# A decoder block on one core: in its first stage the low part of h is subtracted by VectorE from PSUM, GpSimd subtracts 256 columns at a time, and the adaLN sums are issued earlier

## The chip, the cores and the metric

The kernel runs on one core of a Trainium2 chip. The metric is the device time of one execution in microseconds. Before the change three runs gave 889.89, 890.54 and 891.4 us, median 890.54.

## What is computed

The reference is one decoder block for 512 tokens of width 1024, all in float32: RMS norm and adaLN modulation, a projection of width 6656 for two attention branches and their gates, block-sparse attention and retention in parallel, gated merging, output projection, a squared-ReLU MLP and a last RMS norm. The change concerns the first lines alone:

```python
c_act = jax.nn.silu(c)
ada = (c_act @ w_ada[l] + b_ada[l])[:, None, :]
sh1, sc1, g1, sh2, sc2, g2 = jnp.split(ada, N_ADA, axis=-1)
h = modulate(rms_norm(x, ln1_w[l]), sh1, sc1)   # h * (1 + scale) + shift
proj = h @ w_in[l]
mq, mk, mv, rq, rk, rv, rg, ga, gr = jnp.split(proj, split_at, axis=-1)
```

`w_ada` is 1024 x 6144, `w_in` 1024 x 6656.

## The kernel before

To keep float32 accuracy on TensorE, each matrix is split in two parts of type float32r: a high part, which is a rounded copy, and a low part, which is the matrix minus that copy. A product of two matrices is three products: high by high, high by low, low by high. Names that begin with `whi` and `wlo` are the parts of a weight, `hh{j}` and `hl{j}` those of h.

The first stage walks over the 8 chunks j of 128 columns of `x` (the loop `for j in range(NK)`, line 338). For every chunk it needs four things:

- **The modulation.** The 128 shifts and 128 scales of the chunk are columns of silu(c) @ w_ada. `load_ada` brings 1 MB of w_ada as tile `wada` in four loads of 256 KB (3 buffers). The product is taken on VectorE and ScalarE, not on TensorE: `ada_start` (line 261) lets ScalarE write the first two of eight weighted rows as `adaacc`, and `ada_sum` (line 268) adds the other six with VectorE, one instruction of 128 x 256 each (line 270), in two sums that alternate, and then adds the two (line 274). `ada_columns` (line 276) sums over the partitions with four small matmuls into the bank `O`: these are called the column sums below. `modulation` (line 283) makes `mod` of them on VectorE (lines 285 and 286).
- **h.** `transposed` (line 288) lets TensorE turn four 128 x 128 blocks of the normalised x into the bank `PT`, of which there is one. `h_tile` (line 297) lets ScalarE write h to an SBUF tile (line 299), then `hh` as a copy of it (line 224); the low part `hl` is subtracted by GpSimd (line 227, `POOL`), for the last chunk by VectorE.
- **The weights.** `load_first` brings 0.39 MB of w_in as `raw` (128 x 768, 3 buffers): the columns of v, and of the first pairs of heads of q and k. `w_split` (line 302) has `whi` copied by ScalarE (line 304) and `wlo` subtracted by GpSimd in one instruction of 768 columns (line 305). Elsewhere, in `load_w`, GpSimd subtracts 1024 columns in four pieces of 256 (line 187).
- **The products.** `product` (line 345) issues one of 18 matmuls: six outputs (four banks of v, one of q, one of k), each with hh by whi, hh by wlo, hl by whi.

PE, VectorE, ScalarE and GpSimd run this stage in the order in which the program is written (a manual schedule); the loads stand in the queue of SP. In round j, TensorE's order was: transposes of chunk j+1, six products hh by whi, three hh by wlo, the column sums of chunk j+1, three hh by wlo, six hl by whi. Behind the stage PE alone keeps a written order; the other engines' order there is set by a scheduler. The loads of the first pair of later weights (`first_pair`), the split of v (`moba_v`) and the rotary embedding of q and k (`rope`, `stack_q`, `stack_k`, tiles `sw`, `roped`, `sig`, `qs`, `kh`, `kl`) follow, then the attention's first scores (`moba_scores`, lines 563 and 564).

Of the kernel before, what the change touches and what calls it, by code (L numbers as in the profile page):

```python
# [8 lines left out]
F32 = mybir.dt.float32  # L9
F32R = mybir.dt.float32r  # L10
AF = mybir.ActivationFunctionType
ALU = mybir.AluOpType
AX = mybir.AxisListType

P = 128
D = 1024
S = 512
NT = S // P
NK = D // P
# [8 lines left out]
def block_kernel(  # L28
# [27 lines left out]
    ACT, DVE, POOL, PE = nc.scalar, nc.vector, nc.gpsimd, nc.tensor  # L56
# [26 lines left out]
    hh = [H.tile([P, S], F32R, name=f"hh{j}", tag=f"hh{j}") for j in range(NK)]  # L83
    hl = [H.tile([P, S], F32R, name=f"hl{j}", tag=f"hl{j}") for j in range(NK)]
    z_stack, Z = pool("Z", "right")
    vm_stack, VM = pool("VM", "right")
    st_stack, ST = pool("start")
# [54 lines left out]
    cact = G.tile([P, 8], F32, name="cact")  # L142
# [29 lines left out]
    def load_raw(parts):  # L172
# [2 lines left out]
            dma(view(raw), src)  # L175
        return raw

    def load_w(parts, lo_engine=None, pool=G):
        raw = load_raw(parts)
        hi = pool.tile([P, 1024], F32R, name="whi", tag="whi", bufs=4 if pool is G else 2)  # L180
        lo = pool.tile([P, 1024], F32R, name="wlo", tag="wlo", bufs=4 if pool is G else 2)
        ACT.activation(hi, raw, AF.Copy)  # L182
        eng = lo_engine or POOL

        for q in range(0, 1024, 256):
            qs = slice(q, q + 256)
            eng.tensor_sub(lo[:, qs], raw[:, qs], hi[:, qs].bitcast(F32))  # L187
        return hi, lo

    def v3(t, n):  # L190
# [10 lines left out]
    def load_pair(w, k0, ca, cb, lo_engine=None):  # L201

        hi, lo = load_w(
            [
                (lambda t: v3(t, 256)[:, :, 0:P], rows(w, k0, 4, ca, P)),
                (lambda t: v3(t, 256)[:, :, P:256], rows(w, k0, 4, cb, P)),
            ],
            lo_engine=lo_engine,
        )
        return v3(hi, 256), v3(lo, 256)  # L210
# [11 lines left out]
    def split(src, hi, lo, eh, el):  # L222
        if eh is ACT:
            ACT.activation(hi, src, AF.Copy)
        else:
            eh.tensor_copy(hi, src)  # L226
        return el.tensor_sub(lo, src, hi.bitcast(F32)).ins  # L227
# [19 lines left out]
    def load_ada(j):  # L247
        t = ST.tile([P, 8, 2, P], F32, name="wada", tag="wada", bufs=3)
        for k0, k1, i in ((0, 4, 0), (0, 4, 1), (4, 8, 0), (4, 8, 1)):
            dma(t[:, k0:k1, i, :], wada_v[:, k0:k1, i, j * P : (j + 1) * P])  # L250
        return t.rearrange("p k a n -> p k (a n)")

    def load_first(j):
        raw = G.tile([P, 1024], F32, name="raw", tag="raw", bufs=3)
        for c0, c1, src in ((0, 512, MV), (512, 640, MQ), (640, 768, MK)):
            dma(raw[:, c0:c1], w_in[j * P : (j + 1) * P, src : src + c1 - c0])
        hi = G.tile([P, 1024], F32R, name="whi", tag="whi", bufs=4)
        lo = G.tile([P, 1024], F32R, name="wlo", tag="wlo", bufs=4)
        return raw[:, :768], hi[:, :768], lo[:, :768]

    def ada_start(j):

        a = [ST.tile([P, 256], F32, name="adaacc", tag="adaacc", bufs=4) for _ in range(2)]
        for k in range(2):
            ACT.activation(a[k], ada[j][:, k, :], AF.Copy, scale=cact[:, k : k + 1])
        return a

    def ada_sum(j, a, ks, end=True):
        for k in ks:
            DVE.scalar_tensor_tensor(  # L270
                a[k % 2], ada[j][:, k, :], cact[:, k : k + 1], a[k % 2], op0=ALU.mult, op1=ALU.add
            )
        if end:
            DVE.tensor_add(a[0], a[0], a[1])  # L274

    def ada_columns(a):

        cp = ps("O")
        for i in range(2):
            PE.matmul(cp[:, 2 * i : 2 * i + 2], a[0][:, i * P : (i + 1) * P], ones32[:, 0:2], start=True, stop=True)  # L280
        return cp

    def modulation(j, cp):
        mod = ST.tile([P, 2], F32, name="mod", tag="mod", bufs=3)
        DVE.tensor_scalar(mod[:, 0:1], cp[:, 0:1], badac(0, j), None, op0=ALU.add)
        DVE.tensor_scalar(mod[:, 1:2], cp[:, 2:3], badac(1, j, True), ln1c(j), op0=ALU.add, op1=ALU.mult)
        return mod

    def transposed(j):
        tp = ps("PT")  # L290
        for t in range(NT):
            PE.transpose(tp[:, t * P : (t + 1) * P], xt[t][:, j * P : (j + 1) * P], ident)
            if j == 0:
                busy(3)
        return tp

    def h_tile(j, tp, mod):
        h32 = ST.tile([P, S], F32, name="h32", tag="h32", bufs=2)
        ACT.activation(h32, tp, AF.Identity, bias=mod[:, 0:1], scale=mod[:, 1:2])
        split(h32, hh[j], hl[j], ACT, POOL if j < NK - 1 else DVE)  # L300

    def w_split(j):
        raw, hi, lo = wf[j]
        ACT.activation(hi, raw, AF.Copy)
        POOL.tensor_sub(lo, raw, hi.bitcast(F32))

    for t in range(1, NT):
        load_x(t)
        if t == 2:
            load_params()  # L310
    ada, wf = [], []

    def load_step(j):
        ada.append(load_ada(j))
        wf.append(load_first(j))

    for j in range(2):
        load_step(j)
    for t in range(NT):
        ss = ST.tile([P, 1], F32, name="ss", tag="ss", bufs=4)  # L320
        ACT.activation(sq, xt[t], AF.Square, accum_out=ss)
# [5 lines left out]
    a = ada_start(0)  # L327
# [4 lines left out]
    tp = transposed(0)  # L332
    busy(4)
    cp = ada_columns(a)
    busy(3)
    mod = modulation(0, cp)
    w_split(0)
    a = ada_start(1)
    h_tile(0, tp, mod)
    for j in range(NK):  # L340
        _, hi, lo = wf[j]
        more = j + 1 < NK
        if j + 2 < NK:
            load_step(j + 2)

        def product(i, a, b, first, last):

            w = (hi, lo)[b]
            hx = (hh, hl)[a][j]
            if i < 4:  # L350
                PE.matmul(acc_mv[i], hx[:, i * P : (i + 1) * P], w[:, 0:512], start=first, stop=last)
            else:
                c0 = 512 if i == 4 else 640
                PE.matmul((acc_q0, acc_k0)[i - 4], w[:, c0 : c0 + P], hx, start=first, stop=last)

        if more:
            ada_sum(j + 1, a, range(2, 8))
            tp = transposed(j + 1)
        for i in range(6):
            product(i, 0, 0, j == 0, False)  # L360
        for i in range(6):
            product(i, 0, 1, False, False)
            if not more:
                product(i, 1, 0, False, True)
            elif i == 2:
                cp = ada_columns(a)
                mod = modulation(j + 1, cp)
        if more:
            w_split(j + 1)
            if j + 2 < NK:  # L370
                a = ada_start(j + 2)
            else:
                first_pair = [load_pair(w_in, k0, MQ + P, MK + P, eng) for k0, eng in ((0, POOL), (4, DVE))]
            h_tile(j + 1, tp, mod)
            for i in range(6):
                product(i, 1, 0, False, False)
    st_stack.close()
# [905 lines left out]
```

## Time and profile before

| what | value |
|---|---|
| median of 3 runs | 890.54 us |
| the profiled execution, its own time | 889.06 us |
| its span, first to last instruction | 887.0 us |
| mean granted TensorE clock | 0.993 |
| TensorE busy (PE) | 851.1 us, 96% of the span |
| VectorE (DVE), ScalarE (ACT), GpSimd (POOL) busy | 468.0, 408.7, 506.1 us |
| the first stage: first products, last products end | 19.2 us, 70.1 us |

All positions below are microseconds from the start of the span. A row of the timeline gives the start, the time until the end of the last instruction of the row, the engine, the line and operation, what is written from what is read, the number of instructions, and in brackets the idle time before it with what ended it. Instructions of one engine overlap by some 0.1 us, so four in a row take less than four times one. Matmuls overlap more: the rows say 0.39 us for a product of 512 columns, and their starts lie 0.23 us apart. PEclk is the granted clock as a share of 2.4 GHz.

### The profile page before, as it was taken

To read this page: it belongs to the slowest core of one execution; us is meant where nothing else is said; L and a number is where in the kernel's file an instruction comes from. 1 tells how busy PE (TensorE), PEld (TensorE's weight loads), DVE (VectorE), ACT (ScalarE), POOL (GpSimd) and SP (SyncE) were. 2 spreads that over 40 slices of the span, in tenths; PEclk is the share of its full clock that TensorE was granted. 3 is DMA by queue.
4 is the path that set the end of the run, shared out by engine and by line. 5 is a ranking of instruction groups with operands and counts; after the bars stand their busy time and mean duration, and the time that the engine had idled before them with its cause. 6 is when DMAs were issued, how large, how long until landed. Compare 5 with 4: busy or idle time off the path is not lost.

```text
span 887.0 us, 11777 instructions
## 1 busy us (share of the span) xinstructions
PE 851.1 (96%) x4138; PEld 708.8 (80%) x4138; DVE 468.0 (53%) x887; ACT 408.7 (46%) x697; POOL 506.1 (57%) x608
## 2 busy tenths in 40 slices
PE   7889999999999999999999889999999999999996
PEld 4667878779788988778888679888888888888885
DVE  5885676777787877973286786103304022222225
ACT  5457988887645637645232253323332211112125
POOL 4466353526544644655656375977777755555554
PEclk9999999999999999999999999999999999999999
DMA  9945222221354453422454732534433322222202
GB/s 280 297 143 173 65 77 66 96 72 48 119 157 141 120 160 103 147 80 89 132 181 152 251 114 90 156 97 127 137 98 93 113 95 96 97 99 99 107 28 95
DMA packets 104426, 108.41 MB, mean 122 GB/s; under 512 B 4832, under 2 KB 93232, under 8 KB 104368
## 3 DMA queue, kind: packets, MB, share of 16 engines
q1 hardware_dynamic: 104224, 107.41, 38.9%
q8 instruction: 32, 0.52, 0.3%
q14 instruction: 26, 0.21, 0.1%
q10 hardware_dynamic: 144, 0.26, 0.1%
HBM read 105.55 MB, written 2.10 MB: 121 GB/s over the span
## 4 chain that ended last, share of the span: by engine, by line
PE 63%; DVE 18%; ACT 8%; DMA 6%; issue 3%; POOL 1%; SPq 1%; ACTq 0%; DVEq 0%; POOLq 0%
PE ps_acc L218 16%; PE ps_acc L219 16%; PE ps_acc L220 16%; DMA ada_raw<-in_w_ada_dram 4%; DVE adaacc L270 3%; PE ps_S L220 2%; PE ps_S L219 2%; PE ps_S L218 2%; ACT sw L478 1%; DVE ada_acc L802 1%; DVE adaacc L274 1%; DMA wada<-in_w_ada_dram 1%; ACT whi L182 1%; DVE ada_acc L799 1%; DVE qs L502 1%
## 5 line engine op out<-in xcount | busy, mean ns | idle before, releaser
L187 POOL TENSOR_TENSOR wlo<-raw,whi 128x256 fp32r<-128x256 f32 x500 | 387.7, 808 | 254.3 <-ACT whi L182 221.7
L182 ACT ACTIVATE whi<-raw 128x1024 fp32r<-128x1024 f32 x126 | 132.4, 1057 | 186.0 <-PE ps_O L220 104.9
L218 PE MATMUL ps_acc<-hh,whi 128*128 128x512 f32 x304 | 121.5, 400 | 0.0
L220 PE MATMUL ps_acc<-hh,wlo 128*128 128x512 f32 x304 | 119.5, 393 | 0.0
L219 PE MATMUL ps_acc<-hl,whi 128*128 128x512 f32 x304 | 119.4, 393 | 0.0
L219 PE MATMUL ps_acc<-h2l,whi 128*128 128x512 f32 (+1 forms) x288 | 105.5, 366 | 0.9 <-POOL h2l L227 0.6
L218 PE MATMUL ps_acc<-h2h,whi 128*128 128x512 f32 (+1 forms) x288 | 105.5, 366 | 0.0
L220 PE MATMUL ps_acc<-h2h,wlo 128*128 128x512 f32 (+1 forms) x288 | 105.3, 366 | 0.0
L226 DVE CAST fh<-act 128x512 fp32r<-128x512 f32 x32 | 16.1, 509 | 132.5 <-PE ps_O L219 128.0
L220 PEld LDWEIGHTS ps_acc<-hh,wlo 128*128 128x128 f32 x304 | 57.4, 189 | 12.7
L219 PEld LDWEIGHTS ps_acc<-hl,whi 128*128 128x128 f32 x304 | 57.6, 190 | 10.2
L218 PEld LDWEIGHTS ps_acc<-hh,whi 128*128 128x128 f32 x304 | 57.6, 189 | 10.1
L219 PEld LDWEIGHTS ps_acc<-h2l,whi 128*128 128x128 f32 x288 | 54.3, 189 | 9.8 <-POOL h2l L227 0.8
L220 PEld LDWEIGHTS ps_acc<-h2h,wlo 128*128 128x128 f32 x288 | 54.3, 189 | 8.8
L218 PEld LDWEIGHTS ps_acc<-h2h,whi 128*128 128x128 f32 x288 | 54.3, 189 | 8.6
L219 PE MATMUL ps_acc<-wlo,fh 128*128 128x512 f32 (+1 forms) x136 | 52.1, 383 | 0.0
L220 PE MATMUL ps_acc<-whi,fl 128*128 128x512 f32 (+1 forms) x136 | 52.1, 383 | 0.0
L218 PE MATMUL ps_acc<-whi,fh 128*128 128x512 f32 (+1 forms) x136 | 52.1, 383 | 0.0
L799 DVE SCALAR_TENSOR_TENSOR ada_acc<-ada_raw,cact,ada_acc 128x256 f32<-128x256 f32 x48 | 32.9, 685 | 35.8 <-DMA ada_raw<-in_w_ada_dram 35.1
L1134 ACT ACTIVATE relu<-ps_acc 128x512 f32<-128x512 f32 x32 | 18.8, 587 | 66.0 <-PE ps_acc L220 64.5
L775 DVE TENSOR_TENSOR g<-g,ps_acc 128x256 f32<-128x256 f32 x8 | 3.4, 419 | 86.1 <-PE ps_acc L774 86.1
L1135 POOL TENSOR_TENSOR act<-relu 128x512 f32<-128x512 f32 x32 | 34.3, 1071 | 17.2 <-ACT relu L1134 17.2
(284 smaller groups left out, 1897.4 us busy)
## 6 DMA issues: line engine op xcount, KB each, us to landing
raw<-in_w_ff_dram SPq DMA_DIRECT2D x64, 512.0 KB, 3.3
raw<-in_w_in_dram SPq DMA_DIRECT2D x32, 512.0 KB, 3.7
ada_raw<-in_w_ada_dram SPq DMA_DIRECT2D x64, 256.0 KB, 3.1
raw<-in_w_in_dram SPq DMA_DIRECT2D x36, 256.0 KB, 3.5
wada<-in_w_ada_dram SPq DMA_DIRECT2D x32, 256.0 KB, 5.2
x<-in_x_dram SPq DMA_DIRECT2D x8, 512.0 KB, 4.7
raw<-in_w_ret_o_dram SPq DMA_DIRECT2D x8, 512.0 KB, 3.5
dec<-in_k_decay_dram SPq DMA_DIRECT2D x8, 256.0 KB, 4.5
```

The costliest lines, as they stand in the source:

```text
L182: ACT.activation(hi, raw, AF.Copy)
L187: eng.tensor_sub(lo[:, qs], raw[:, qs], hi[:, qs].bitcast(F32))
L218: PE.matmul(o, lh, rh, start=first, stop=False)
L219: PE.matmul(o, lh, rl, start=False, stop=False)
L220: PE.matmul(o, ll, rh, start=False, stop=last)
L226: eh.tensor_copy(hi, src)
L270: DVE.scalar_tensor_tensor(a[k % 2], ada[j][:, k, :], cact[:, k : k + 1], a[k % 2], op0=ALU.mult, op1=ALU.add)
L274: DVE.tensor_add(a[0], a[0], a[1])
L478: ACT.activation(sw[q0 : q0 + 32, :], a[q1 : q1 + 32, :], AF.Copy)
L799: eng.scalar_tensor_tensor(acc, raw[:, 0, :], cact[:, 2 * k2 : 2 * k2 + 1], acc, op0=ALU.mult, op1=ALU.add)
L1134: ACT.activation(r, a, AF.Relu)
L1135: POOL.tensor_mul(act[n], r, r)
```

## The change

Five things are changed, all in the first stage.

1. ScalarE writes h back into the bank `PT` instead of an SBUF tile, and copies `hh` from there. The tile `h32` is gone.
2. `hl` is subtracted by VectorE, from the bank `PT` and `hh` (`h_low`), for every chunk. GpSimd has no part in it. Only then is the bank free for the next transposes.
3. `wlo` of the first stage is subtracted in three pieces of 256 columns (`sub_pieces`).
4. TensorE's order: the six products hh by whi of chunk j come first, then the transposes and the column sums of chunk j+1, then six hh by wlo and six hl by whi.
5. The sum for chunk j+2 is issued in the program's round j, right behind `h_tile(j+1)`. For chunks 1 to 3 (`ada_ahead`) ScalarE's two rows come behind `hh`, and VectorE takes the other six as a third sum of its own, one product and three multiply-adds in a chain, before it adds to ScalarE's two, with two adds at the end. For chunks 4 to 7 `ada_start` and `ada_sum` are used as before. `adaacc` has 6 buffers instead of 4.

```diff
+    def sub_pieces(eng, lo, src, hi):
+        for c0 in range(0, src.shape[1], 256):
+            cs = slice(c0, c0 + 256)
+            eng.tensor_sub(lo[:, cs], src[:, cs], hi[:, cs].bitcast(F32))
...
     def h_tile(j, tp, mod):
-        h32 = ST.tile([P, S], F32, name="h32", tag="h32", bufs=2)
-        ACT.activation(h32, tp, AF.Identity, bias=mod[:, 0:1], scale=mod[:, 1:2])
-        split(h32, hh[j], hl[j], ACT, POOL if j < NK - 1 else DVE)
+        ACT.activation(tp, tp, AF.Identity, bias=mod[:, 0:1], scale=mod[:, 1:2])
+        ACT.activation(hh[j], tp, AF.Copy)
+
+    def h_low(j, tp):
+        DVE.tensor_sub(hl[j], tp, hh[j].bitcast(F32))
 
     def w_split(j):
         raw, hi, lo = wf[j]
         ACT.activation(hi, raw, AF.Copy)
-        POOL.tensor_sub(lo, raw, hi.bitcast(F32))
+        sub_pieces(POOL, lo, raw, hi)
...
+    def ada_ahead(j, between=None):
+        a = ada_start(j)
+        b = ST.tile([P, 256], F32, name="adaacc", tag="adaacc", bufs=6)
+        DVE.tensor_scalar(b, ada[j][:, 2, :], cact[:, 2:3], None, op0=ALU.mult)
+        for k in range(3, 8):
+            d = b if k < 6 else a[k - 6]
+            DVE.scalar_tensor_tensor(d, ada[j][:, k, :], cact[:, k : k + 1], d, op0=ALU.mult, op1=ALU.add)
+            if k == 3 and between:
+                between()
+        DVE.tensor_add(a[0], a[0], a[1])
+        DVE.tensor_add(a[0], a[0], b)
+        return a
+
+    sums[1] = ada_ahead(1, lambda: h_low(0, tp))
     for j in range(NK):
...
-        if more:
-            ada_sum(j + 1, a, range(2, 8))
-            tp = transposed(j + 1)
         for i in range(6):
             product(i, 0, 0, j == 0, False)
+        ahead = j + 2 < NK
+        if more:
+            tp = transposed(j + 1)
+            mod = modulation(j + 1, ada_columns(sums.pop(j + 1)))
         for i in range(6):
             product(i, 0, 1, False, False)
             if not more:
                 product(i, 1, 0, False, True)
-            elif i == 2:
-                cp = ada_columns(a)
-                mod = modulation(j + 1, cp)
         if more:
             w_split(j + 1)
-            if j + 2 < NK:
-                a = ada_start(j + 2)
-            else:
+            if not ahead:
                 first_pair = [load_pair(w_in, k0, MQ + P, MK + P, eng) for k0, eng in ((0, POOL), (4, DVE))]
+            early = ahead and j >= 2
+            if early:
+                sums[j + 2] = ada_start(j + 2)
             h_tile(j + 1, tp, mod)
+            if early:
+                ada_sum(j + 2, sums[j + 2], range(2, 8))
+            elif ahead:
+                sums[j + 2] = ada_ahead(j + 2)
+            h_low(j + 1, tp)
             for i in range(6):
                 product(i, 1, 0, False, False)
```

The order of instructions on the engines tells what this moves. First VectorE, one round of the later chunks before the change (the end of one sum, the modulation, the next sum):

```order
L274 TENSOR_TENSOR adaacc<-adaacc 128x256
L285 TENSOR_SCALAR mod<-ps_O,cols 128x1
L286 TENSOR_SCALAR mod<-ps_O,cols_143,cols 128x1
L270 SCALAR_TENSOR_TENSOR adaacc<-wada,cact,adaacc 128x256 x6
L274 TENSOR_TENSOR adaacc<-adaacc 128x256
```

The same round in the changed kernel:

```order
L306 TENSOR_TENSOR hl_76<-ps_PT,hh_68 128x512
L288 TENSOR_SCALAR mod<-ps_O,cols 128x1
L289 TENSOR_SCALAR mod<-ps_O,cols_143,cols 128x1
L273 SCALAR_TENSOR_TENSOR adaacc<-wada,cact,adaacc 128x256 x6
L277 TENSOR_TENSOR adaacc<-adaacc 128x256
L306 TENSOR_TENSOR hl_77<-ps_PT,hh_69 128x512
```

Between the sum and the next modulation VectorE now has hl; the sum itself stands where it stood, behind the modulation of the chunk before. For chunks 2 and 3 the sum is the longer form:

```order
L289 TENSOR_SCALAR mod<-ps_O,cols_143,cols 128x1
L349 TENSOR_SCALAR adaacc<-wada,cact 128x256
L352 SCALAR_TENSOR_TENSOR adaacc<-wada,cact,adaacc 128x256 x5
L355 TENSOR_TENSOR adaacc<-adaacc 128x256
L356 TENSOR_TENSOR adaacc<-adaacc 128x256
L306 TENSOR_TENSOR hl_74<-ps_PT,hh_66 128x512
```

One instruction more than before the change stands there, besides hl.

Second TensorE, in the round of chunk 1, before (`x_91` to `x_94` are the four tiles of x, `hh_65` and `hl_73` the parts of chunk 1):

```order
L292 MATMUL ps_PT<-ident,x_91 128x128
L292 MATMUL ps_PT<-ident,x_92 128x128
L292 MATMUL ps_PT<-ident,x_93 128x128
L292 MATMUL ps_PT<-ident,x_94 128x128
L351 MATMUL ps_acc<-whi,hh_65 128x512 x3
L351 MATMUL ps_S<-whi,hh_65 128x512
L354 MATMUL ps_S<-hh_65,whi 128x512 x2
L351 MATMUL ps_acc<-wlo,hh_65 128x512 x3
L280 MATMUL ps_O<-ones_102,adaacc 128x2 x2
L351 MATMUL ps_S<-wlo,hh_65 128x512
L354 MATMUL ps_S<-hh_65,wlo 128x512 x2
```

and in the changed kernel:

```order
L373 MATMUL ps_acc<-whi,hh_65 128x512 x3
L373 MATMUL ps_S<-whi,hh_65 128x512
L376 MATMUL ps_S<-hh_65,whi 128x512 x2
L295 MATMUL ps_PT<-ident,x_91 128x128
L295 MATMUL ps_PT<-ident,x_92 128x128
L295 MATMUL ps_PT<-ident,x_93 128x128
L295 MATMUL ps_PT<-ident,x_94 128x128
L283 MATMUL ps_O<-ones_102,adaacc 128x2 x2
L373 MATMUL ps_acc<-wlo,hh_65 128x512 x3
L373 MATMUL ps_S<-wlo,hh_65 128x512
L376 MATMUL ps_S<-hh_65,wlo 128x512 x2
```

The transposes went behind the six products of the chunk's own high part, and the column sums right behind the transposes, with twelve products after them instead of nine.

Third ScalarE at the start of the attention, before (`whi` is here a weight of the following projections, `sw` the halves that the rotary embedding swaps):

```order
L478 ACTIVATE sig<-ps_S 32x512 x2
L182 ACTIVATE whi<-raw 128x1024
L501 ACTIVATE qs<-roped 64x512
L182 ACTIVATE whi<-raw 128x1024
L501 ACTIVATE qs<-roped 64x512
L518 ACTIVATE kh<-sig 64x512
L519 ACTIVATE kh<-sig 64x512
```

and in the changed kernel:

```order
L505 ACTIVATE sig<-ps_S 32x512 x2
L188 ACTIVATE whi<-raw 128x1024
L528 ACTIVATE qs<-roped 64x512 x2
L505 ACTIVATE sw<-ps_acc 32x512 x2
L545 ACTIVATE kh<-sig 64x512
L546 ACTIVATE kh<-sig 64x512
L188 ACTIVATE whi<-raw 128x1024
```

The second weight copy went behind the first two copies of kh, and a pair of swaps in front of them; this is the scheduler's doing, not the diff's. SP's order and TensorE's order behind the stage are unchanged.

## Rows read from the trace of the kernel before

**Rows 1.** Stretches: us, busy time of each engine (instructions), granted clock, DMA share, GB/s

```profile
24.00:31.40 7.40, 7.40 (x32) 6.09 (x32) 6.09 (x12) 2.94 (x5) 3.50 (x2) 0.77 1.16 299
...
44.50:51.00 6.50, 5.22 (x27) 4.12 (x26) 5.70 (x10) 2.95 (x5) 3.45 (x2) 1.00 0.54 159
...
85.18:89.30 4.12, 4.12 (x13) 3.21 (x12) 1.74 (x4) 1.72 (x5) 2.20 (x6) 0.59 0.58 171
```

**Rows 2.** Chain of waits, first stage: start, us, engine, tile, line

```profile
36.99 0.59 PE ps_O L280 x4
...
37.93 3.51 DVE adaacc L270 x6
...
41.46 1.94 DVE adaacc L274
...
63.18 0.58 PE ps_O L280 x4
```

**Rows 3.** Timeline of GpSimd in the same round

```profile
39.65 1.50 POOL L227 TENSOR_TENSOR hl<-h,hh 128x512 fp32r<-128x512 f32 x1 [3.09 <-ACT hh L224]
41.11 2.00 POOL L305 TENSOR_TENSOR wlo<-raw,whi 128x768 fp32r<-128x768 f32 x1
```

**Rows 4.** Timeline of VectorE while GpSimd stands still

```profile
14.01 1.68 DVE L270 SCALAR_TENSOR_TENSOR adaacc<-wada,cact,adaacc 128x256 f32<-128x256 f32 x4 [0.27 <-DMA wada<-in_w_ada_dram]
15.72 0.43 DVE L274 TENSOR_TENSOR adaacc<-adaacc 128x256 f32<-128x256 f32 x1
```

**Rows 5.** Timeline of GpSimd, eight pieces of 256 columns in a row

```profile
70.14 5.63 POOL L187 TENSOR_TENSOR wlo<-raw,whi 128x256 fp32r<-128x256 f32 x8 [2.90 <-issue]
```

**Rows 6.** Timeline of VectorE during those pieces

```profile
74.47 0.69 DVE L539 TENSOR_TENSOR vm<-ps_acc,vm 128x512 fp32r<-128x512 f32 x1
```

**Rows 7.** Timeline of TensorE: transposes, products of the last chunk, end of the stage

```profile
39.60 0.60 PE L292 MATMUL ps_PT<-ident,x 128*128 128x128 f32 x4
39.95 0.94 PE L351 MATMUL ps_acc<-whi,hh 128*128 128x512 f32 x3
...
65.81 0.96 PE L351 MATMUL ps_acc<-whi,hh 128*128 128x512 f32 x3
...
69.85 0.39 PE L354 MATMUL ps_S<-hl,whi 128*128 128x512 f32 x1
70.08 0.39 PE L218 MATMUL ps_acc<-hh,whi 128*128 128x512 f32 x1
```

**Rows 8.** Timeline of ScalarE in one round (VectorE's first multiply-add: 31.39)

```profile
31.59 0.78 ACT L299 ACTIVATE h<-ps_PT,mod 128x512 f32<-128x512 f32 x1 [3.62 <-DVE mod L286]
32.41 0.63 ACT L224 ACTIVATE hh<-h 128x512 fp32r<-128x512 f32 x1
32.94 0.83 ACT L304 ACTIVATE whi<-raw 128x768 fp32r<-128x768 f32 x1
33.68 0.89 ACT L265 ACTIVATE adaacc<-wada,cact 128x256 f32<-128x256 f32 x2
```

**Rows 9.** Timeline of GpSimd and VectorE, both in pieces of 256 columns

```profile
62.71 3.36 POOL L187 TENSOR_TENSOR wlo<-raw,whi 128x256 fp32r<-128x256 f32 x4
...
64.12 2.58 DVE L187 TENSOR_TENSOR wlo<-raw,whi 128x256 fp32r<-128x256 f32 x4
66.62 0.68 DVE L227 TENSOR_TENSOR hl<-h,hh 128x512 fp32r<-128x512 f32 x1
```

**Rows 10.** Timeline of TensorE: the column sums of chunk 1

```profile
23.81 0.65 PE L280 MATMUL ps_O<-ones,adaacc 128*128 128x2 f32 x4 [2.23 <-DVE adaacc L274]
```

**Rows 11.** Timeline of VectorE in the first step

```profile
17.49 5.81 DVE L270 SCALAR_TENSOR_TENSOR adaacc<-wada,cact,adaacc 128x256 f32<-128x256 f32 x6 [0.18 <-ACT adaacc L265]
```

**Rows 12.** Timeline of ScalarE at the start of the attention

```profile
80.93 1.06 ACT L182 ACTIVATE whi<-raw 128x1024 fp32r<-128x1024 f32 x1 [1.09 <-PE ps_acc L219]
```

**Rows 13.** Timeline of TensorE at the start of the attention

```profile
84.00 0.50 PE L563 MATMUL ps_S<-kh,qs 128*128 128x512 f32 x1 [1.52 <-ACT kh L519]
84.84 0.50 PE L564 MATMUL ps_S<-kl,qs 128*128 128x512 f32 x1 [0.34 <-DVE kl L523]
```

More of the change, by code (lines that the diff above doesn't have):

```diff
@@ L183, in load_w @@
         eng = lo_engine or POOL
-        for q in range(0, 1024, 256):
-            qs = slice(q, q + 256)
-            eng.tensor_sub(lo[:, qs], raw[:, qs], hi[:, qs].bitcast(F32))
+        sub_pieces(eng, lo, raw, hi)
         return hi, lo
@@ L261, in ada_start @@
     def ada_start(j):
-        a = [ST.tile([P, 256], F32, name="adaacc", tag="adaacc", bufs=4) for _ in range(2)]
+        a = [ST.tile([P, 256], F32, name="adaacc", tag="adaacc", bufs=6) for _ in range(2)]
         for k in range(2):
@@ L310, in block_kernel @@
             load_params()
[L311 to L318, printed above, removed]
+    ada = [load_ada(0)]
+    wf = [load_first(0)]
+    ada.append(load_ada(1))
+    wf.append(load_first(1))
+    ada.append(load_ada(2))
     for t in range(NT):
@@ L337, in block_kernel @@
     w_split(0)
-    a = ada_start(1)
     h_tile(0, tp, mod)
+    sums = {}
+    def ada_ahead(j, between=None):
[11 more added lines that the diff above has]
+    sums[1] = ada_ahead(1, lambda: h_low(0, tp))
     for j in range(NK):
@@ L343, in block_kernel @@
         if j + 2 < NK:
-            load_step(j + 2)
+            wf.append(load_first(j + 2))
+        if j + 3 < NK:
+            ada.append(load_ada(j + 3))
         def product(i, a, b, first, last):
```

## The prediction

> **What bounds the kernel now.** I began with the table of stretches. In the first stage TensorE was busy 5.22 of 6.50 us, although the transfers had nearly run out there (159 GB/s against 299 earlier) [rows 1]: neither TensorE nor the DMA sets the pace. The chain of waits names who does. From the column sums of one step (36.99) to those of the last (63.18) lie four equal rounds, 6.55 us each, and TensorE appears in them only with the four small matmuls of the column sums; the rest is VectorE, six multiply-adds in 3.51 us and one add in 1.94 us [rows 2]. The timeline of GpSimd explains those two: hl runs 39.65 to 41.15, wlo 41.11 to 43.11 [rows 3]. Where GpSimd stands still, four multiply-adds take 1.68 us and the same add 0.43 [rows 4], so one multiply-add costs 0.48, five ahead of it 0.40 each, and six should cost 2.46. In the round the sixth ended 0.3 us behind GpSimd's hl and the add 0.3 us behind its wlo: a VectorE instruction with two operands in SBUF waits until GpSimd's running instruction is over. The stage is bound by GpSimd's two long instructions inside VectorE's chain.
>
> **The change part by part.** The words "a step ahead" move less than they say. On VectorE the sums of step j+1 still stand between the modulations of steps j and j+1. What is new there is hl behind the sum; on TensorE the transposes and column sums come three products earlier; and GpSimd loses hl and gets three short pieces for one long wlo.
>
> *Short rounds (column sums 3 to 7, four of them).* From column sums to the first multiply-add 0.94 (36.99 to 37.93) [rows 2]. Six multiply-adds 2.46, a gap of 0.03, the add 0.43 [rows 4], a gap of 0.03. Then hl from PSUM, 0.69: a VectorE instruction of this size with one operand in PSUM took 0.69 while GpSimd ran eight pieces in 5.63, that is 0.70 each without a delay [rows 5, 6], so hl is not held by GpSimd. The transposes cannot start before hl, since it reads the only PT bank: 0.05 of wait and 0.35 for four of them (39.60 to 39.95) [rows 7]. Together 4.98. Now the pieces: ScalarE begins h 0.20 behind the first multiply-add, ends hh at 1.65 and whi at 2.38 [rows 8], so the first piece takes its operands at about 2.4, when the add wants to at 2.5. Four VectorE pieces that met two GpSimd pieces took 2.58 against 1.68 [rows 4, 9], 0.45 for each piece met. I take one piece met: 5.43. The ends: none met, and then TensorE's own work decides, 18 products of 0.23, the transposes and at most 0.59 of column sums, 5.1 [rows 2, 7]; or all three met, 6.3. Four rounds save 4 x (6.55 - 5.43) = **4.5** (1.0 to 5.8).
>
> A page speaks against reading h from PSUM. The Trainium skill, Perfetto Trace Analysis, section Optimizing Scalar/DVE Operations, gives VectorE about 60 ns of overhead on SBUF and 125 on PSUM, so by it hl would be 0.07 dearer in each of the four rounds and the saving 4.2. The rows have 0.68 for hl from SBUF and 0.69 for its like from PSUM [rows 6, 9]; they decide.
>
> Another speaks about the pieces. The Trainium skill, SBUF — State Buffer, section Who interferes with whom, says that the loser is blocked for the whole instruction of the other; by it a piece met would cost up to its 0.70 and the four rounds would save 3.5. The 0.45 of the rows is for instructions that already waited part of it beside their own start; I keep it.
>
> *Long rounds (column sums 1 to 3, two of them).* Here the sum is one product, three multiply-adds that each wait for the one before (0.48 and 0.03 of gap), two that wait for ScalarE's pair, and two adds. That pair now runs behind hh: 1.65 to 2.55 behind the first VectorE instruction [rows 8]. The last multiply-add ends at 3.1, the adds at 3.5 and 4.0, hl at 4.7, the transposes at 5.1; with 0.94 that is 6.05. whi ends at 3.4, so one piece meets the second add: 6.5. Before, the two took 36.99 - 23.81 = 13.18 [rows 2, 10]. Saving **0.2** (from 1.1 to a loss of 0.7, with no piece or two met in each).
>
> *First step.* The six multiply-adds took 5.81 [rows 11], among GpSimd's wlo, hl and wlo. The new sum is longer alone by about 1.1 (a dependent chain, one more add) and has hl in its middle, but only short pieces to meet. I take **0.3** earlier, between 0.6 and nothing.
>
> *End of the stage.* Between the last column sums and hh of the last step TensorE has twelve products where it had nine. It had no slack there (63.18 to 65.81, nine products) [rows 2, 7], so three products of 0.23 are added, less 0.1 that it waited: a loss of **0.6** (0.5 to 0.7).
>
> *Transfers.* SP's order is unchanged. A load of wada needs the buffer of the sum three steps before; the last waits until sum 4 has read its own, which was at 41.44 [rows 2] and will be near 40. Sum 7 starts only near 53, so nothing waits for that load. Before it the loads run at 299 GB/s [rows 1] for 1.44 MB a step (four of 256 KB, and 0.39 MB of w_in), 4.8 us, less than a short round. The extra buffers only take memory.
>
> *Start of the attention.* The scheduler put a swap pair and the first kh pair ahead of a weight copy on ScalarE, which had waited 1.09 us for TensorE there and took 1.06 [rows 12]; the first scores wait for kh and kl until 84.84 [rows 13]. The scores can come up to 1.1 earlier, or 0.1 later (a swap pair of 1.2 for a copy of 1.06). VectorE gets roped, 0.69, ahead of kl, so I take **0.5** earlier.
>
> Everything behind keeps TensorE's order and is busy with it, so I cost it at nothing. If VectorE's small reorderings there are not covered, each is worth one instruction, some 0.7.
>
> Sum: 0.3 + 0.2 + 4.5 - 0.6 + 0.5 = **4.9 us**. The profiled execution took 889.06 and would take 884.2. It lies 1.5 below the median of the three runs, 890.54, on which I put the forecast: **885.6**.
>
> **The rivals.**
> *TensorE sets the round.* If the add slips in ahead of the first piece (it wants the operands within 0.1 of it), a round is 5.1, and four rounds save 1.3 more: 884.3. With it may come the clock. After 24.0 the granted clock was 0.77 in the mean, and after 85.18 it was 0.59 [rows 1]: the lower level, 1.2 GHz, for 3.4 us each time, behind idle stretches of 2.2 us (up to 23.81) and 1.9 us (up to 84.84, with one product in it) [rows 10, 13], while the 1.3 us gaps of the rounds left it at 1.00. If the second idle stretch shrinks enough, half of 3.4 comes back, 1.7: down to 882.6 with both. For it: the shorter wait there; against it: most of that stretch remains.
>
> *The pieces stay in the chain.* All three met in each short round: 6.3, and only 0.9 is left of 4.5. Then 889.2, no change that counts. Against it: whi ends when five of six multiply-adds are through [rows 8].
>
> *The PT bank turns into the bound.* Sum, hl, transposes, column sums and modulation now form one ring through one bank. If each of three pieces held VectorE for its full 0.70 inside this ring, a short round would be 4.98 + 2.1 = 7.1 and a long one 8.15: four times 0.55 and 3.1 for the two lost, with the tail 5.9, and 0.8 gained elsewhere. That gives 895.6, slower. It decides at a ring of 6.55, that is from 1.6 us of holding in a short round. For it: transposes ran ahead of the sum before, and cannot now; against it: the 0.45 of the pieces met [rows 9].
>
> *The change does not do what it says.* VectorE's order shows that no sum is earlier than it was. If the length of the sum and not GpSimd had set the round, nothing would be saved and the tail lost: 891. The lone add of 0.43 against 1.94 speaks against it [rows 2, 4].
>
> **How the numbers follow.** A run of this kernel can be told from no change at about 0.2%, 1.8 us. The forecast with one piece met has 0.62, from 883.5 to 887.5 by the bounds of the long rounds, the first step and the attention start. TensorE's round with or without the clock 0.19 (882.0 to 884.3); pieces in the chain 0.10; no sum earlier 0.04; the bank 0.05. Faster by over 0.2% takes the first two and a little of the third, 0.84; within 0.2% takes most of the third and fourth, 0.11; slower 0.05. The range leaves out the ring, the fourth case and half of the third above, and the deepest of the clock's case below: 882.5 to 888.4.
>
> **What would show it.** Right: column sums 3 to 7 5.3 to 5.5 apart; no GpSimd row of hl; wlo in pieces of 0.70 to 0.9; the add at 0.9 in place of 1.94; hl at 0.69 right behind it; transposes right behind hl; the first column sums of the long rounds still 6.5 apart; the stage's end near 65.6 in place of 70.08. Wrong: hl longer than 0.8 beside GpSimd, two or more VectorE instructions of a round above 0.8, ScalarE's copies of h dearer in PSUM than 0.78 and 0.63, TensorE idle at the start of the attention longer than before, or time lost behind 90 us, where nothing was foreseen.

## The result and the profile after

The changed kernel took 883.99 us (median of four runs, 882.88 to 885.55), the kernel before 890.21 on the same chip: a ratio of 0.993, with a 95% interval from 0.991 to 0.995. It is faster by 6.2 us. The profiled execution took 882.88, its span is 881.0 in place of 887.0.

The stretches answer to [rows 1]: us, busy time of each engine (PE, PEld, DVE, ACT, POOL, with instructions), granted clock, DMA share, GB/s. The first is one short round of the changed kernel, the second the start of the attention, the third a place far behind the change.

```profile
35.33:40.81 5.48, 5.20 (x29) 4.15 (x27) 4.28 (x10) 2.88 (x5) 2.30 (x4) 1.00 1.11 300
79.25:83.40 4.15, 4.15 (x20) 3.46 (x19) 3.79 (x9) 2.39 (x6) 2.94 (x4) 1.00 0.44 126
520.50:523.90 3.40, 3.40 (x16) 3.40 (x17) 3.37 (x6) 0.70 (x1) 1.75 (x2) 0.50 0.41 104
```

A short round lasts 5.47 us where it lasted 6.55, and TensorE is busy in 95% of it. Behind the scores the granted clock is 1.00, where it was 0.59 [rows 1]. On the other hand it is 0.50, 1.2 GHz, for 3.4 us from 520.5, a fall that the profile of before has not. No run shows that the two have to do with each other.

The chain of waits through one short round, which answers to [rows 2]:

```profile
47.15 2.46 DVE adaacc L273 x6
...
49.63 0.91 DVE adaacc L277
50.54 0.61 DVE hl L306
...
51.29 0.63 PE ps_PT L295 x4
51.92 0.35 PE ps_O L283 x4
```

The six multiply-adds have gone from 3.51 to 2.46 and the add from 1.94 to 0.91. hl and the transposes have come into the chain, as the two rows between the add and the column sums. VectorE still sets the round. Its timeline, with GpSimd's first piece and ScalarE's two copies of the same round, shows what holds it now; these rows answer to [rows 3, 4, 8]:

```profile
36.20 2.46 DVE L273 SCALAR_TENSOR_TENSOR adaacc<-wada,cact,adaacc 128x256 f32<-128x256 f32 x6
38.69 0.91 DVE L277 TENSOR_TENSOR adaacc<-adaacc 128x256 f32<-128x256 f32 x1
39.52 0.68 DVE L306 TENSOR_TENSOR hl<-ps_PT,hh 128x512 fp32r<-128x512 f32 x1
...
38.57 0.74 POOL L182 TENSOR_TENSOR wlo<-raw,whi 128x256 fp32r<-128x256 f32 x1 [3.18 <-ACT whi L310]
...
36.38 0.75 ACT L302 ACTIVATE ps_PT<-ps_PT,mod 128x512 f32<-128x512 f32 x1 [2.58 <-DVE mod L289]
37.16 0.60 ACT L303 ACTIVATE hh<-ps_PT 128x512 fp32r<-128x512 f32 x1
```

The first piece starts 0.12 us ahead of the add and runs until 39.31; the add ends at 39.60. hl then runs beside the second piece and takes 0.68, as it did from SBUF.

TensorE, and ScalarE at the start of the attention; these rows answer to [rows 7, 10, 12, 13]:

```profile
22.65 0.49 PE L283 MATMUL ps_O<-ones,adaacc 128*128 128x2 f32 x3 [0.58 <-DVE adaacc L356]
...
40.34 0.63 PE L295 MATMUL ps_PT<-ident,x 128*128 128x128 f32 x4 [0.28 <-DVE hl L306]
40.81 0.51 PE L283 MATMUL ps_O<-ones,adaacc 128*128 128x2 f32 x4
...
64.54 0.39 PE L221 MATMUL ps_acc<-hh,whi 128*128 128x512 f32 x1
...
77.67 0.49 PE L590 MATMUL ps_S<-kh,qs 128*128 128x512 f32 x1 [0.73 <-ACT kh L546]
78.91 0.50 PE L591 MATMUL ps_S<-kl,qs 128*128 128x512 f32 x1 [0.75 <-DVE kl L550]
...
74.98 1.19 ACT L505 ACTIVATE sw<-ps_acc 32x512 f32<-32x512 f32 x2
76.33 0.63 ACT L545 ACTIVATE kh<-sig 64x512 fp32r<-64x512 f32 x1 [0.16 <-DVE sig L517]
76.99 0.63 ACT L546 ACTIVATE kh<-sig 64x512 fp32r<-64x512 f32 x1
77.64 1.06 ACT L188 ACTIVATE whi<-raw 128x1024 fp32r<-128x1024 f32 x1
```

The stage ends at 64.54 in place of 70.08, 5.5 us earlier; that is nearly all of the gain. The two stops of TensorE ahead of the scores are 0.73 and 0.75 in place of 1.52 and 0.34, and ScalarE has the swap pair (`sw`) and kh ahead of the weight copy. Behind the scores the lead grows to 7.5 us, since TensorE keeps its clock; of that 1.5 are given back by the end, about 0.4 of it near 110 us, and most of the rest around 500 to 530 us, where the fall of the third stretch lies.

### The profile page after: what moved, and what is told of

Same layout as the page of the kernel before. It is cut to its first block, busy times and chain, and to the rows that moved or that the text cites. A ratio compares the mean times of both kernels' runs of the same rounds, so it can differ in the third digit from the quotient of the medians.

```text
span 881.0 us, 11795 instructions
## 1 busy us (share of the span) xinstructions
PE 849.6 (96%) x4138; PEld 708.5 (80%) x4138; DVE 460.4 (52%) x897; ACT 408.1 (46%) x697; POOL 499.2 (57%) x617
## 4 chain that ended last, share of the span: by engine, by line
PE 67%; DVE 15%; ACT 7%; DMA 7%; issue 3%; POOL 1%; SPq 0%; ACTq 0%; DVEq 0%; POOLq 0%
PE ps_acc L221 17%; PE ps_acc L222 17%; PE ps_acc L223 17%; DMA ada_raw<-in_w_ada_dram 3%; DMA wada<-in_w_ada_dram 2%; PE ps_S L223 2%; PE ps_S L222 2%; PE ps_S L221 2%; ACT sw L505 1%; DVE ada_acc L829 1%; DVE ada_acc L826 1%; DVE qs L529 1%; ACT whi L188 1%; PE ps_PT L223 1%; PE ps_PT L222 1%
## 5 line engine op out<-in xcount | busy, mean ns | idle before, releaser
L182 POOL TENSOR_TENSOR wlo<-raw,whi 128x256 fp32r<-128x256 f32 x524 | 407.2, 809 | 277.6 <-ACT whi L188 222.5
```

The source lines that it names most:

```text
L182: eng.tensor_sub(lo[:, cs], src[:, cs], hi[:, cs].bitcast(F32))
```

## The experiments

The theory was that GpSimd's long instructions stood inside VectorE's chain and that this was the whole bound of the stage. Each run takes one part out of the change, does one part alone, or adds what the theory says is next. Times are medians, with the ratio to the kernel before on the same chip; the spacings are those of the column sums (`PE ps_O`) in the profiled execution.

| kernel | us | ratio (95%) | first step | long rounds | short round |
|---|---|---|---|---|---|
| before | 890.2 | | 7.52 | 6.72, 6.46 | 6.55 |
| changed | 884.0 | 0.993 (0.991 to 0.995) | 6.71 | 6.39, 6.29 | 5.47 |
| changed, wlo whole | 891.4 | 1.001 (1.000 to 1.002) | 8.80 | 8.04, 7.37 | 6.57 |
| changed, hl on GpSimd | 891.0 | 1.000 (0.999 to 1.001) | 7.49 | 7.12, 7.08 | 5.46 |
| before, with pieces only | 884.9 | 0.994 (0.992 to 0.996) | 7.26 | 8.33, 5.39 | 5.46 |
| changed, column sums first | 882.2 | 0.991 (0.989 to 0.992) | 7.41 | 5.32, 5.38 | 4.97 |
| changed, plain sums | 880.9 | 0.989 (0.987 to 0.991) | 5.91 | 5.02, 5.46 | 5.47 |
| both of the last two | 878.9 | 0.987 (0.986 to 0.989) | 4.79 | 5.24, 4.96 | 4.96 |
| the changed one, six pieces | 882.5 (one run) | | 6.17 | 6.72, 6.01 | 5.19 |

### wlo in one instruction again

```diff
     def w_split(j):
         raw, hi, lo = wf[j]
         ACT.activation(hi, raw, AF.Copy)
-        sub_pieces(POOL, lo, raw, hi)
+        POOL.tensor_sub(lo, raw, hi.bitcast(F32))
```

> The changed kernel with wlo of the first stage in one GpSimd instruction of 768 columns again. Theory one (GpSimd's long instruction inside VectorE's chain is what the change took away): the instruction of 2.0 us starts about 0.1 us ahead of the add, the add ends some 0.3 us behind it, so a short round goes from 5.47 to 6.5 or 6.7 us and the long rounds lose 0.6 to 1.0 each; the time is 888.5 to 890. Theory two (what counts is that hl left GpSimd, the pieces are small change): short rounds stay within 0.3 us of 5.47 and the time within 1.5 us of the changed kernel's 884.

Measured: 891.37 us, and short rounds of 6.57. VectorE's and GpSimd's timeline of one of them:

```profile
48.41 2.46 DVE L273 SCALAR_TENSOR_TENSOR adaacc<-wada,cact,adaacc 128x256 f32<-128x256 f32 x6
50.91 2.00 DVE L277 TENSOR_TENSOR adaacc<-adaacc 128x256 f32<-128x256 f32 x1
...
50.79 1.83 POOL L311 TENSOR_TENSOR wlo<-raw,whi 128x768 fp32r<-128x768 f32 x1 [4.80 <-DMA raw<-in_w_in_dram]
```

The add waits out the 768 columns: 2.00 in place of 0.91, which is 1.09 of the 1.10 by which the round is longer. Without the pieces the rest of the change gains nothing. The time is 1.4 us above the bound given, since the first step and the long rounds lost more than foreseen; the granted clock was at its lower level for 10.2 us there, and how much of that loss is the clock's the run does not tell.

### hl back on GpSimd

```diff
+        h32 = ST.tile([P, S], F32, name="h32", tag="h32", bufs=2)
-        ACT.activation(tp, tp, AF.Identity, bias=mod[:, 0:1], scale=mod[:, 1:2])
-        ACT.activation(hh[j], tp, AF.Copy)
+        ACT.activation(h32, tp, AF.Identity, bias=mod[:, 0:1], scale=mod[:, 1:2])
+        ACT.activation(hh[j], h32, AF.Copy)
+        h32s.append(h32)
...
     def h_low(j, tp):
-        DVE.tensor_sub(hl[j], tp, hh[j].bitcast(F32))
+        (POOL if j < NK - 1 else DVE).tensor_sub(hl[j], h32s[j], hh[j].bitcast(F32))
```

> The changed kernel with h in SBUF again and hl of chunks 0 to 6 on GpSimd, behind the pieces of wlo; the order on TensorE, the sums and the pieces stay. Theory one (the pieces do it): the sixth multiply-add waits for hl until about 3.1 us behind the first, the add then meets one piece; hl (0.69) and the transposes (0.35) are out of VectorE's ring. A short round is 5.2 to 5.6 us and the time 883 to 885.5, no different from the changed kernel. Theory two (moving hl does it): VectorE is held about 1 us more in each round, short rounds are 6.3 to 6.6 us and the time is 887.5 to 889.

Measured: short rounds of 5.46, as theory one had it, and yet 891.0 us, 5.5 above its range. VectorE in a long round (the first row) and in a short one, and GpSimd in the short one:

```profile
25.59 3.87 DVE L356 SCALAR_TENSOR_TENSOR adaacc<-wada,cact,adaacc 128x256 f32<-128x256 f32 x5
...
39.38 3.50 DVE L273 SCALAR_TENSOR_TENSOR adaacc<-wada,cact,adaacc 128x256 f32<-128x256 f32 x6
42.92 0.84 DVE L277 TENSOR_TENSOR adaacc<-adaacc 128x256 f32<-128x256 f32 x1
...
41.10 1.49 POOL L310 TENSOR_TENSOR hl<-h,hh 128x512 fp32r<-128x512 f32 x1 [3.09 <-ACT hh L304]
42.56 2.47 POOL L182 TENSOR_TENSOR wlo<-raw,whi 128x256 fp32r<-128x256 f32 x3
```

In a short round hl on GpSimd holds the six multiply-adds for 1.04 us (3.50 against 2.46); on VectorE it costs its own 0.68 and puts the transposes, 0.35, into the ring. That is the same, so moving hl saves nothing there. In the first step and the long rounds, where the five multiply-adds take 3.87 in place of 2.49, it costs 0.8 each: 2.3 us in the three. The attention starts as before the change, with a stop of 1.53 us ahead of the scores and the clock at its lower level for 3.4 us behind it:

```profile
82.10 0.50 PE L594 MATMUL ps_S<-kh,qs 128*128 128x512 f32 x1 [1.53 <-ACT kh L550]
...
82.90:86.30 3.40, 3.26 (x8) 2.58 (x9) 0.71 (x3) 1.62 (x3) 2.65 (x6) 0.50 0.53 155
```

Set beside the profile of the changed kernel, this one is 3.1 us later at the last column sums (the 2.3, and 0.8 by which its first column sums came later), 4.1 at the scores with kl, and 5.6 behind the fall of the clock. It makes up about 1 us of that by the end, 0.6 of it where the changed kernel's clock falls at 520.5, and takes 887.30 against 882.88. The median, 3.7 above this execution, does not follow from these terms, so the same kernel was run again. Nor does that median measure the move of hl alone, since the order at the start of the attention went back with it.

> The kernel with hl back on GpSimd once more, one look, since its profiled execution (887.3) lay 3.7 us below the median of its ten runs. Theory one (the usual execution has more stretches at the lower clock): at least two more falls of the granted clock than in the first profile, each costing 1 to 1.7 us, with the first stage as long as there. Theory two (the first stage itself varies by some us from run to run): the same falls, and the end of the stage more than 2 us later.

Measured: 889.78 us, with the same rounds (7.49, 7.09, 7.11, 5.47). Two of its stretches at the lower clock are not in the first profile:

```profile
33.10:36.50 3.40, 3.40 (x10) 2.63 (x9) 3.16 (x5) 3.30 (x7) 2.12 (x3) 0.51 1.16 300
...
497.30:500.70 3.40, 3.40 (x9) 2.64 (x9) 0.00 (x0) 0.00 (x0) 0.81 (x1) 0.50 1.06 409
```

Theory one, with its price only half right: the fall at 33.1 cost nothing, since VectorE set that round. The 2.2 us more stand between the scores and the end. The fall at 497.3 cost 1.6; near 344 us, where the clock did not fall, another 0.9 was lost, and 0.3 was made up elsewhere. Over the ten runs of this kernel the mean granted clock lay between 0.984 (891.29 us) and 0.994 (887.30). What makes the clock fall in one execution and not in the next stays open, and with it the rest of that median.

### The pieces alone

The edit is made in the kernel before, in `w_split`:

```diff
-        POOL.tensor_sub(lo, raw, hi.bitcast(F32))
+        for q in range(0, 768, 256):
+            qs = slice(q, q + 256)
+            POOL.tensor_sub(lo[:, qs], raw[:, qs], hi[:, qs].bitcast(F32))
```

> The kernel before, with nothing but wlo of the first stage in three pieces of 256 columns. Theory one: six multiply-adds still take 3.5 us (hl on GpSimd holds the sixth), the add 0.9 in place of 1.94; a short round is 5.4 to 5.6 us, and without the three products more at the end of the stage the time is 885 to 886.5, some 4 to 5 us faster than before. Theory two (hl has to leave GpSimd): the second and third piece hold the add as one long instruction did, short rounds stay above 6.2 us and the time above 888.5.

Measured: 884.92 us, ratio 0.994, short rounds of 5.46. VectorE in a short round, and the stretch that made one long round 8.33:

```profile
39.00 3.50 DVE L270 SCALAR_TENSOR_TENSOR adaacc<-wada,cact,adaacc 128x256 f32<-128x256 f32 x6
42.53 0.85 DVE L274 TENSOR_TENSOR adaacc<-adaacc 128x256 f32<-128x256 f32 x1
...
24.40:31.20 6.80, 6.80 (x20) 5.63 (x21) 4.65 (x9) 2.94 (x5) 3.81 (x4) 0.50 1.15 301
```

Theory one: hl still holds the multiply-adds, the add has fallen from 1.94 to 0.85, and the time, just below the range given, is that of the changed kernel within the intervals. One line of the change, three pieces for one instruction, does what all five parts do together. (The profiled execution was the slowest of five, 888.44. In it TensorE at 1.2 GHz set the second round, and the clock fell again at 495.5 and 526.2 us.)

### The column sums ahead of the transposes

```diff
-            tp = transposed(j + 1)
-            mod = modulation(j + 1, ada_columns(sums.pop(j + 1)))
+            cp = ada_columns(sums.pop(j + 1))
+            tp = transposed(j + 1)
+            mod = modulation(j + 1, cp)
```

> The changed kernel with the column sums ahead of the transposes on TensorE. Theory one (VectorE's ring through the one PT bank sets the round): the column sums no longer wait for hl and 0.35 us of transposes lie beside the modulation, so a short round falls from 5.47 to 4.9 or 5.1 us, where TensorE's own work (18 products of 0.23, the transposes, the column sums) sets it; the time is 0.9 to 2.2 us below the changed kernel, 882 to 883. Theory two (TensorE already sets the round, or ScalarE's h then waits for the transposes): rounds stay within 0.1 us of 5.47 and the time at 883.5 to 884.5.

Measured: 882.2 us, short rounds of 4.97. Two rounds as a stretch:

```profile
45.01:54.93 9.92, 9.92 (x53) 8.43 (x52) 8.56 (x20) 5.91 (x9) 4.60 (x7) 1.00 0.81 220
```

Theory one. TensorE is busy in all of the stretch: the bound has gone from VectorE's ring to TensorE. hl and the transposes no longer stand between the add and the column sums, and a round is 0.5 us shorter, which is all that TensorE's own work allows.

### Plain sums for chunks 1 to 3

```diff
+    sums = {1: ada_start(1)}
     h_tile(0, tp, mod)
-    sums = {}
...
-    sums[1] = ada_ahead(1, lambda: h_low(0, tp))
+    ada_sum(1, sums[1], range(2, 8))
+    h_low(0, tp)
...
-            early = ahead and j >= 2
+            early = ahead
```

> The changed kernel with the sums of chunks 1 to 3 written like those of the later chunks (ScalarE's pair ahead of h, six multiply-adds, one add); all else stays. Theory one (the long rounds are long because of the dependent chain and the second add): both long rounds fall from 6.39 and 6.29 to 5.4 to 5.7 us, the first step stays within 0.7 of its 6.7, and the time is 1 to 2 us below the changed kernel's 884, 882 to 883. Theory two (the transfers of wada or the pair ahead of h set these rounds): they stay above 6.1 us, and the time at 884 or above.

Measured: 880.91 us, 3 us below the changed kernel, more than either theory had. VectorE in the first long round:

```profile
23.33 2.46 DVE L273 SCALAR_TENSOR_TENSOR adaacc<-wada,cact,adaacc 128x256 f32<-128x256 f32 x6
25.82 0.43 DVE L277 TENSOR_TENSOR adaacc<-adaacc 128x256 f32<-128x256 f32 x1
26.16 0.68 DVE L306 TENSOR_TENSOR hl<-ps_PT,hh 128x512 fp32r<-128x512 f32 x1
```

The long form with ScalarE's pair behind hh (`ada_ahead`) cost 0.8 us in the first step and 2.2 in the two rounds. ScalarE's pair ahead of h did not delay h, which starts at 23.51, 0.18 behind VectorE's first multiply-add, as it does in the changed kernel (36.38 and 36.20).

### Both

The column sums first and plain sums together, in two runs.

> The changed kernel with both edits: the column sums ahead of the transposes on TensorE (the kernel of the earlier run of that edit alone, 882.2) and the sums of chunks 1 to 3 written like the later ones. Theory one (the long rounds of that kernel, 5.32 and 5.38, are VectorE's longer sum; the rest is TensorE's): all rounds from the first column sums on are 4.9 to 5.1 us, the first step falls by 0.5 to 1.7, and the time is 880 to 881.5. Theory two (TensorE and the transfers already set these rounds): rounds above 5.2 remain and the time is within 0.6 of 882.2.

> The kernel with column sums ahead of the transposes and plain sums once more, beside the next one on the same chip. Theory one (its lead over the changed kernel is real): ratio to before 0.985 to 0.989 again. Theory two (luck of the first run): above 0.991.

Measured: 878.86 and 878.13 us, ratios 0.987 and 0.988 (intervals 0.986 to 0.989 and 0.986 to 0.990). This is the version that beats both kernels: 11.3 us under the one before, 5 under the changed one. Five rounds as a stretch, and what VectorE waits for in the second of them:

```profile
26.63:51.50 24.87, 24.87 (x131) 21.09 (x130) 20.94 (x51) 16.15 (x26) 11.59 (x17) 1.00 1.12 301
```

```profile
33.81 1.67 DVE L273 SCALAR_TENSOR_TENSOR adaacc<-wada,cact,adaacc 128x256 f32<-128x256 f32 x4 [0.39 <-DMA wada<-in_w_ada_dram]
```

TensorE stands still nowhere, and the transfers run at 301 GB/s throughout; VectorE already waits 0.39 us for one. One of the two long rounds stayed at 5.24, against theory one; the first step fell by more than it had, 7.41 to 4.79, and took the time below its range.

### Matmuls into the idle stretch of the kernel before

Six products that nothing reads are added to the kernel before:

```diff
     fill(9)
+    idle = ps("O")
+    for _ in range(6):
+        PE.matmul(idle, ones, hh[0], start=True, stop=True)
     for t in (3, 2, 1, 0):
         moba_scores(0, t)
```

> The kernel before with six more matmuls (ones by hh of chunk 0, 512 columns, into the free bank of the O tag, never read) on TensorE in the idle stretch ahead of the attention's first scores. Theory one (the granted clock falls to its lower level there because TensorE stands still for 1.9 us from the last product's start; the kernels whose stretch is 1.1 us keep it): the stretch is filled, the granted clock stays at 1.00 from 28 us to beyond 400 us, the products behind the scores take 0.39 in place of 0.63, and the time is 1.3 to 1.8 us below before. Theory two (the clock falls whatever stands in that stretch, or because of the second gap, between the two scores): it falls within 3 us of the scores again, and the time is within 0.4 us of before.

Measured: 889.8 us, ratio 0.9995 (0.999 to 1.000): not the gain of theory one. The stretch behind the scores, then TensorE's timeline and one row of ScalarE's:

```profile
86.74:90.80 4.06, 4.06 (x20) 3.37 (x19) 1.66 (x4) 1.62 (x5) 2.21 (x6) 1.00 0.57 170
```

```profile
83.87 1.56 PE L891 MATMUL ps_O<-hh,ones 128*128 128x512 f32 x6
85.55 0.50 PE L563 MATMUL ps_S<-kh,qs 128*128 128x512 f32 x1
86.40 0.50 PE L564 MATMUL ps_S<-kl,qs 128*128 128x512 f32 x1 [0.36 <-DVE kl L523]
...
92.37 0.50 PE L218 MATMUL ps_acc<-hh,whi 128*128 128x512 f32 x1 [0.98 <-ACT sw L478]
...
91.13 1.19 ACT L478 ACTIVATE sw<-ps_acc 32x512 f32<-32x512 f32 x2
```

The clock did stay at 1.00 with TensorE kept at work, so that half of theory one holds. Of the 1.5 us that it gained on the kernel before between the scores and 89 us, 1.1 were waited for right behind: a product at 92.37 needs a bank that ScalarE's swap copies (`sw`) are still reading. The rest was lost in waits by 118 us. In the changed kernel a pair of these copies stands ahead of kh, and no such wait follows: its lead of 7.5 us stands from 90 to 109 us, so the gain of the clock is kept there.

### One piece of a projection more ahead of the scores

The edit is made in the kernel with both edits:

```diff
-    fill(9)
+    fill(10)
     for t in (3, 2, 1, 0):
...
-    fill(1)
```

> The kernel of e7_again with one piece of the next projection more (six products, 1.36 us) ahead of the attention's first scores, and one less behind the first four. Theory one (the two stops there, 1.1 and 1.25 us from start to start, are lost time on TensorE): one stop of at most 0.4 us is left and the time falls by 0.8 to 1.4 us. Theory two (what is gained there is waited for later, since the scores, and with them the softmax, start 0.5 us later): TensorE waits longer at the first products by th (1.48 us before them now), and the time stays within 0.5 us.

Measured: 877.32 us beside 878.13, no difference that can be told. The stop at kh is gone, the one at kl is 0.38, and a new one stands behind:

```profile
73.99 0.50 PE L593 MATMUL ps_S<-kl,qs 128*128 128x512 f32 x1 [0.38 <-DVE kl L552]
...
89.38 0.66 PE L623 MATMUL ps_PT<-ident,pr 128*128 128x128 f32 x4 [1.39 <-ACT pr L610]
```

Theory two in kind: the 1.4 us gained at the scores are all waited for by 89.4 us, but at the transposes of the softmax's result, not at the products by th.

### Six pieces

```diff
-        sub_pieces(POOL, lo, raw, hi)
+        for c0 in range(0, 768, 128):
+            cs = slice(c0, c0 + 128)
+            POOL.tensor_sub(lo[:, cs], raw[:, cs], hi[:, cs].bitcast(F32))
```

> The changed kernel with wlo of the first stage in six pieces of 128 columns. Theory one (the add waits for the one piece that runs when it wants to start, and ends 0.3 us behind it): a piece takes about 0.4 us, the add 0.55 to 0.65 in place of 0.91, a short round 5.1 to 5.25 us in place of 5.47, four of them 0.9 to 1.4 us less. Theory two (each piece met costs the same whatever its length, or the add meets a second one): the add takes 0.85 or more and a short round stays at 5.4 or above.

Measured: short rounds of 5.19. The add, and GpSimd's first piece:

```profile
39.57 0.63 DVE L277 TENSOR_TENSOR adaacc<-adaacc 128x256 f32<-128x256 f32 x1
...
39.45 0.46 POOL L313 TENSOR_TENSOR wlo<-raw,whi 128x128 fp32r<-128x128 f32 x1 [2.48 <-ACT whi L310]
```

Theory one: the piece is over at 39.91, the add at 40.20. Its price over the 0.43 of a free add is 0.20 here, 0.48 with 256 columns and 1.57 with 768. In the three rounds shown the piece began 0.12 us ahead of the add, and the add ended 0.29 us behind it.

## Why the prediction was right

The forecast was 885.6, the range 882.5 to 888.4; measured were 883.99. Against its profiled execution it said 4.9 us less, and there were 6.2 (889.06 to 882.88). By its own steps:

- **Short rounds, 4.5 forecast, 4.3 measured** (4 x 1.08). A round was to be 5.43 and is 5.47: six multiply-adds of 2.46 (2.46 forecast), one piece met by the add at 0.48 (0.45), hl at 0.68 (0.69) and not held beside a piece. This was the step that carried the sum. The Trainium skill, SBUF — State Buffer, section Who interferes with whom, says that a VectorE instruction with two inputs in SBUF contends with GpSimd's reads, and that one with at most one such input, outside VectorE's two-port modes, does not. The trace agrees on both: the add with 0.91, hl with 0.68. The section says of the two-port modes that whoever is first keeps the ports for its whole instruction; here the six pieces and the whole wlo show the same for the add, and what it is worth: what is left of GpSimd's instruction when VectorE arrives.
- **The other page.** The Trainium skill, Perfetto Trace Analysis, section Optimizing Scalar/DVE Operations, gives figures from which the prediction worked out an estimate: hl dearer from PSUM by 0.07. It took 0.68 from PSUM here and 0.68 from SBUF [rows 9]; the trace does not show that difference at this size.
- **Long rounds, 0.2 forecast, 0.5 measured** (13.18 to 12.68). As described, the second add met a piece (0.85). Inside the bounds.
- **First step, 0.3 forecast, 1.2 measured**: mis-sized. 0.4 of it lies ahead of the change, at the first column sums (15.93 for 16.29), which came anywhere from 15.93 to 17.63 in the kernels run. The step itself is 0.8 shorter: the bound of 0.6 was too low. Its two adds met single pieces (0.84 and 0.83), where the multiply-adds had met a whole wlo and hl (5.81 [rows 11]).
- **End of the stage, a loss of 0.6 forecast, 0.4 measured** (6.90 to 7.32 from the last column sums).
- **Start of the attention, 0.5 forecast, 0.4 measured**, by the scores with kl: 78.91 is 14.37 behind the stage's end, where it was 14.76. Those with kh came 0.8 earlier, kl followed later.
- **The clock, 0 forecast, 1.6 measured.** The prediction tied it to the rival in which TensorE sets the round. It came without that: with stops of 0.73 and 0.75 us in place of 1.52 and 0.34 the clock did not fall. The filler run supports the reason, the stop, as do the other profiles: the clock fell there in all four with a stop of 1.52 or 1.53 us and in none of the other nine. The filler run also shows that such a gain can vanish in the next waits. This is the largest term that the sum lacked.
- **Behind 91 us nothing was foreseen**, and 1.5 us were lost there, one of the prediction's own signs of being wrong. That these 1.5 and the clock's 1.6 nearly cancel is luck.

The rivals: TensorE does not set the round in the changed kernel (0.28 us of wait remain), but does once the column sums go first, at 4.97 where 5.1 was worked out. The pieces stay in the chain, one of three. The ring through the PT bank exists, and at 5.47 stays below the 6.55 from which it would have decided. The length of the sum did not set the round: the same six multiply-adds and add fell from 5.45 to 3.37 us.

What the number hides is how the parts share the gain. The prediction let hl's move and the pieces save together; the runs show that the pieces alone give the 6 us, that the move of hl is worth nothing in a short round, and that the new form of the first sums costs 3 us which the other parts win back. With that form in place, putting hl back on GpSimd took the whole gain away (891.0); the traces account for 2.3 us in the first step and the long rounds and about 2.5 from there to the fall of the clock behind the scores, and the rest stays open. The move of hl alone, without pieces, in the kernel before was not tried, nor was TensorE's new order taken out by itself.

## What to carry to other kernels

Where VectorE's and GpSimd's instructions took two operands from SBUF, the wait was the rest of the running instruction: cut the one that is off the path into pieces, first and by itself. When several edits go together, take each out once, since one may be paying for another. A stop of TensorE that is filled, or a clock that is kept, is worth something only if the next wait behind it also moves.

## What the runs showed of the hardware

- VectorE's add that started 0.12 us behind a GpSimd subtraction ended 0.29 us after it, for 128, 256 and 768 columns alike, and took 0.63, 0.91 and 2.00 us.
- GpSimd's subtraction of 128 columns took 0.46, of 256 columns 0.74 and of 768 columns 1.83 us when nothing but this add met it.
- ScalarE took 0.75 us for h of 128x512 from PSUM into PSUM, where it took 0.78 into SBUF, and 0.60 for hh from PSUM, where it took 0.63 from SBUF [rows 8].
- At the scores the granted clock fell to 1.2 GHz behind stops of 1.52 and 1.53 us (before, pieces alone, hl on GpSimd twice). It stayed at 2.4 GHz in the seven profiles with two stops of 0.72 to 0.75 us, with one of 0.38, and with the six matmuls in the stop.
